# A two-layer hybrid step on one core: the recurrent unit's branch is computed two tiles ahead, and at attention's end an output cast moves between two key casts and more of the projection is offered early

## The chip, the cores and the metric

One core of a Trainium2 chip. The metric is the device time of one execution in microseconds (us), as the median of several runs.

## What is computed

The reference is one inference step through two layers on 640 tokens of width 1024, of which 512 are latent tokens on a grid of 8 rows by 64 columns and 128 are prompt tokens. Layer 0 mixes by neighbourhood attention with 16 heads of 64 (latent queries also read 256 cached and the prompt's keys in one softmax; the prompt attends to itself); layer 1 mixes by a recurrent unit. Behind each mixer comes a feed-forward of width 2816, ahead of each part a root-mean-square norm with a shift and a scale from the conditioning, and behind it a gated add to the residual.

The recurrent unit, per channel of 1024, is:

```
y  = gelu(x @ wi_gate)
xr = x @ wi_branch;  xc = conv4(xr)            # centred, depthwise, bias
r, i = sigmoid(gate matrices (128x128 blocks) @ xc), for both directions
a  = exp(-8 r softplus(-lam));  b = sqrt(1 - a^2) * (i * xc)
h  = a * h + b      # one scan forward, one backward, from given states
out = (y * (h_fwd + h_bwd)) @ wlo
```

## The kernel before

**Precision and chunks.** Every large product is made of float32 numbers split in two: a high part (a cast to the reduced type, on ScalarE) and a low part (the remainder, a subtraction on VectorE). For each of eight slices k of the contraction three matmuls are issued: high by high (line 221), high by low (222), low by high (223). The tokens lie along the free axis, in two halves (320 and 320, or 384 and 256 in the recurrent unit), so a chunk, that is one output tile of 128 channels by one half, is 24 matmuls (`chunk` and `some`). The order in which the engines get their instructions is decided when the program is built, by a scheduler that starts from the order of the code; `pin` sets an instruction behind another.

**Weights and banks.** `unit` loads a weight tile (`raw`), casts it (line 180, `whi` or `whx`) and subtracts (line 182, `wlo` or `wlx`). In the recurrent unit the high part comes by a DMA on the POOL queue. `pg` hands out the accumulators: three banks `mm`, and, where a stage has `mx` banks, those at two of every five calls (`ng % 5` of 1 or 3). So each call of `pg` shifts the turn for all later ones. `ps` gives a named bank, and the stage's first one where the name isn't there.

**Attention's end.** The heads go in eight pairs p. While p = 6 is attended, `qk` makes queries and keys of pair 7: `QS` and `KS` are casts (line 799), one for each head of the pair, and `KZ` the key's remainder (line 800). Behind these the output `O` of the pairs 0 to 6 is split into `ohi` and `olo` (`split`, lines 1313 and 1315), and TensorE begins the output projection (`project`, with `ahead`), three chunks of it early, in slices that fill the waits of the last softmax. That softmax runs through line 830 (scores with their bias and maximum), 833 (exponent), 837 and 839 (scale), 842 (transposes to `tp`), 844 (copies) and 922 (output `op`); for the prompt through 859 to 872. Line 929 copies `op` to `O`. Slice 7 of the output is split last.

**The recurrent unit.** Eight tiles f of 128 channels. `lru_xr` makes the branch in two chunks and copies it, with columns ahead of rows, to one of two buffers `xr` (line 1251). `lru_a` runs the convolution (its first tap on ScalarE, line 1259, three more on VectorE, line 1261) to one of two buffers `xc`, then the gate matrices on TensorE in four pieces (line 1271, `gp`, two buffers), each followed by a tanh that frees its banks (line 1272, ScalarE). `lru_b` makes the coefficients: exponent and tanh (1283, 1284), square root (1285), products (1286, 1287). `lru_c` scans in both directions (1296) and adds the two (1303, 1304). `lru_gate` makes the gate in two chunks and its gelu (1323 to 1327). `lru_d` multiplies (1308) and splits the result (1313, 1315). Tanh, root and gelu are in different tables, so ScalarE loads a table at each turn (ACT_TABLE_LOAD). The loop over t issues `lru_a` of tile t, the branch of t + 1, `lru_b` of t − 1, `lru_c`, the gate and `lru_d` of t − 2.

**The second feed-forward.** Its norm has a second statistic: ones times squares on TensorE (543, 546, tile `at`), variance on VectorE (548), a power on GpSimd (550), a diagonal matrix on VectorE (552), and its spread over the partitions by TensorE into an `mx` bank (560). Around it stand the feed-forward's first chunks (lines 1142 to 1144).

Of the kernel before, what the change touches and what calls it, by code (L numbers as in the profile page):

```python
# [125 lines left out]
class _Step:  # L126
# [467 lines left out]
    def project(self, w, hi, lo, gk, nxt=None, done=None, ahead=False):  # L594
        G = self.need(self.gcols, gk)
        for f in range(KT):
            u = self.unit(w[f], "m" if ahead else None)
            for t0, t1 in CH:
                self.residual(f, t0, t1, self.chunk(u, hi, lo, t0, t1, not ahead or f > 1), G, nxt)
                if nxt:  # L600
                    self.scale(f, t0, t1, *nxt)
            if done:
                done(f)
        if nxt:
            self.stats()
            self.shift(*nxt)
# [173 lines left out]

    def qk(self, p, hi, lo, ap, Q=None, K=None):
        nc = self.nc
# [12 lines left out]
        for S, v, lo in pairs if p else pairs[::-1]:  # L795
            for a in range(2):
                hp = slice(a * HD, a * HD + HD)
                op = slice(HD - a * HD, P - a * HD)
                cast = nc.scalar.copy(S[hp, a], v[hp]).ins
                low = nc.vector.tensor_tensor(lo[a][hp], v[hp], S[hp, a].bitcast(F32), ALU.subtract).ins  # L800
                queue = nc.gpsimd if p in (0, 7) else nc.sync
                queue.dma_start(S[op, a].bitcast(F32), Q[hp] if v is Q else S[hp, a].bitcast(F32))
        self.parted = low, cast
        return QS, KS, KZ
# [448 lines left out]

    def lru_a(self, f, lp):
        nc, xr = self.nc, self.xrs[f % 2]
        gw = self.t([P, 2, 2, P], F32, "gw", 2, lp)
        nc.sync.dma_start(gw, self.i["wg"][f])
        xc = self.t([P, LW], F32, "xc", 2, lp)
        nc.scalar.activation(xc, xr[:, 0:LW], AF.Identity, scale=self.col("cw0", f), bias=self.col("cb", f))
        for j in range(1, 4):  # L1260
            nc.vector.scalar_tensor_tensor(xc, xr[:, j:j + LW], self.col(f"cw{j}", f), xc, ALU.mult, ALU.add)

        def lt():
# [74 lines left out]
    def run(self):  # L1338
# [35 lines left out]
        with self.phase("attn", tp=2, sp=2, op=1, quota=24) as ap:  # L1374
# [10 lines left out]
            for p in range(8):  # L1385
# [3 lines left out]
                new = []  # L1389
                self.attend(p, *QK, V, O, ap, (lambda: new.extend(self.qk(7, xhi, xlo, ap))) if p == 6 else None)  # L1390
                if p == 5:
# [5 lines left out]
                if p == 6:  # L1397
                    ohi = self.big()
                    olo = self.big()
                    for k in range(KT - 1):  # L1400
                        self.split(ohi[:, k], olo[:, k], O[:, k], self.parted)
# [21 lines left out]
        with self.phase("lru", at=1) as lp:  # L1423
            A, B, C, G = {}, {}, {}, {}
            self.xrs = [self.t([P, 648], F32, f"xr{j}", 1, lp) for j in range(2)]
            for xr in self.xrs:
# [61 lines left out]
```

## Time and profile before

| | |
|---|---|
| median of three runs | 1521.86 us (1520.55 to 1522.31) |
| the profiled execution | 1522.37 us |
| its span | 1520.6 us |
| TensorE (PE) busy | 1491.2 us, 98% of the span |
| VectorE (DVE) busy | 1061.5 us, 70% |
| ScalarE (ACT) busy | 698.1 us, 46% |
| GpSimd (POOL) busy | 261.4 us, 17% |
| attention's end (slices of the output projection between the last scores) | about 290 to 320 us of the span |
| recurrent unit's tiles | about 905 to 1030 us |

A row of the order of events holds its start, its length, the engine, the line, the operation, the tile written and the tiles read, the shape, and the count of instructions merged in it; in brackets the idle time of that engine before it, with the engine, tile and line that ended it. The idle time of PE is what counts here. PEclk in a window is the mean clock that TensorE was granted, as a share of full speed. The length of a row holds the pipeline's run-out too, so the next row may start before it is over.

### The profile page before, as it was taken

The numbers are of one execution on the slowest core, as the hardware profiler recorded it, in microseconds if no ns is written. First come the engines' busy times: TensorE is split into PE (matmuls) and PEld (weight loads), VectorE is DVE, ScalarE is ACT, GpSimd is POOL, SyncE is SP. The second block draws the span as 40 slices with busy tenths as digits, with TensorE's granted clock in tenths as the row PEclk, the third lists the DMA queues.
The fourth block names the chain that finished last, engine by engine and source line by source line (L and its number), as shares of the span: only waits on it lengthen the run. The fifth ranks groups of instructions, "written<-read, shape, count | busy, mean of one in ns | idle before, by whom it ended". The sixth has DMA issues, their size and how long they took to land. (4 is left out here: it accounts for less than half of the span.)

```text
span 1520.6 us, 26116 instructions
## 1 busy us (share of the span) xinstructions
PE 1491.2 (98%) x10373; PEld 1441.8 (95%) x10373; DVE 1061.5 (70%) x2005; ACT 698.1 (46%) x1268; POOL 261.4 (17%) x276
## 2 busy tenths in 40 slices
PE   8999999999999999999999999899999999999997
PEld 5999999889999999999999887799999999999997
DVE  5778998679999997434443769876975655566555
ACT  4676766654332123312321478764644342434243
POOL 0112132100111110000000014230232323222211
PEclk9999999999999999999999999999999999999999
DMA  9644665446556664222222543316242231323211
GB/s 375 174 143 160 186 189 167 117 139 194 176 185 195 207 196 132 62 84 84 65 73 83 150 134 102 119 59 216 70 156 80 74 111 57 100 67 97 71 56 70
DMA packets 72330, 196.65 MB, mean 129 GB/s; under 512 B 8048, under 2 KB 24592, under 8 KB 72080
## 3 DMA queue, kind: packets, MB, share of 16 engines
q1 hardware_dynamic: 57392, 142.32, 29.6%
q0 software_dynamic: 14240, 51.98, 11.1%
q8 instruction: 81, 1.33, 0.4%
q10 hardware_dynamic: 576, 0.68, 0.1%
q14 instruction: 41, 0.34, 0.1%
HBM read 179.48 MB, written 8.92 MB: 124 GB/s over the span
## 5 line engine op out<-in xcount | busy, mean ns | idle before, releaser
L221 PE MATMUL mm<-big,whi 128*128 128x320 f32 (+3 forms) x1233 | 383.9, 313 | 4.0 <-ACT big L1313 2.8
L222 PE MATMUL mm<-big,whi 128*128 128x320 f32 (+3 forms) x1233 | 384.2, 312 | 1.7 <-DVE big L1315 1.3
L223 PE MATMUL mm<-big,wlo 128*128 128x320 f32 (+3 forms) x1233 | 384.1, 312 | 0.2 <-DVE wlo L182 0.2
L221 PEld LDWEIGHTS mm<-big,whi 128*128 128x128 f32 x1233 | 233.0, 189 | 6.7 <-ACT big L1313 3.5
L222 PEld LDWEIGHTS mm<-big,whi 128*128 128x128 f32 x1233 | 233.6, 189 | 3.8 <-DVE big L1315 2.2
L223 PEld LDWEIGHTS mm<-big,wlo 128*128 128x128 f32 x1233 | 233.2, 189 | 1.6 <-DVE wlo L182 0.4
L250 DVE SCALAR_TENSOR_TENSOR mprod<-mraw,csb 128x1024 f32<-128x1024 f32 x160 | 194.9, 1218 | 11.8 <-DMA mraw<-in_wm 11.4
L590 DVE SCALAR_TENSOR_TENSOR x<-mm,G,x 128x320 f32<-128x320 f32 (+2 forms) x192 | 77.8, 435 | 82.4 <-PE mm L223 82.3
L180 ACT CAST whi<-raw 128x1024 fp32r<-128x1024 f32 (+1 forms) x71 | 73.9, 1041 | 113.9 <-PE mm L222 65.6
L182 DVE TENSOR_TENSOR wlo<-raw,whi 128x1024 fp32r<-128x1024 f32 (+1 forms) x87 | 105.9, 1218 | 28.7 <-ACT whi L180 16.5
L221 PE MATMUL mm<-big,whx 128*128 128x320 f32 (+3 forms) x348 | 108.4, 311 | 0.0
L223 PE MATMUL mm<-big,wlx 128*128 128x320 f32 (+3 forms) x348 | 108.0, 310 | 0.0
L222 PE MATMUL mm<-big,whx 128*128 128x320 f32 (+3 forms) x348 | 107.9, 310 | 0.0
L246 POOL DMA_DIRECT2D mraw<-in_wm x80 | 43.0, 537 | 358.6 <-DVE mprod L250 266.0
L221 PE MATMUL mx<-big,whi 128*128 128x320 f32 (+3 forms) x287 | 89.5, 312 | 0.0
L223 PE MATMUL mx<-big,wlo 128*128 128x320 f32 (+3 forms) x287 | 88.9, 310 | 0.0
L222 PE MATMUL mx<-big,whi 128*128 128x320 f32 (+3 forms) x287 | 88.7, 309 | 0.0
L221 PE MATMUL mx<-big,whx 128*128 128x320 f32 (+3 forms) x260 | 80.6, 310 | 0.0
L223 PE MATMUL mx<-big,wlx 128*128 128x320 f32 (+3 forms) x260 | 80.5, 310 | 0.0
L180 ACT CAST whx<-raw 128x1024 fp32r<-128x1024 f32 (+1 forms) x40 | 41.1, 1029 | 85.9 <-PE mm L222 47.3
L222 PE MATMUL mx<-big,whx 128*128 128x320 f32 (+3 forms) x260 | 80.3, 309 | 0.0
L1313 ACT CAST whi<-raw 128x1024 fp32r<-128x1024 f32 (+1 forms) x41 | 41.3, 1008 | 70.3 <-PE mm L222 45.2
(347 smaller groups left out, 3725.3 us busy)
## 6 DMA issues: line engine op xcount, KB each, us to landing
raw<-in_gu SPq DMA_DIRECT2D x88, 512.0 KB, 3.5
mraw<-in_wm POOLq DMA_DIRECT2D x80, 512.0 KB, 3.9
raw<-in_dn SPq DMA_DIRECT2D x24, 512.0 KB, 3.6
sw<-in_wm SPq DMA_DIRECT2D x16, 512.0 KB, 10.7
raw<-in_wqk SPq DMA_DIRECT2D x16, 512.0 KB, 4.8
raw<-in_wi SPq DMA_DIRECT2D x16, 512.0 KB, 3.5
whi<-in_wi POOLq DMA_DIRECT2D x16, 512.0 KB, 3.9
raw<-in_dn SPq DMA_DIRECT2D x16, 448.0 KB, 3.3
```

The lines of the kernel that those rows point to most:

```text
L180: nc.scalar.copy(hi, raw)
L182: nc.vector.tensor_tensor(lo, raw, hi.bitcast(F32), ALU.subtract)
L221: nc.tensor.matmul(ps, hi[:, k], xhi[:, k, s], start=(k == 0), stop=False)
L222: nc.tensor.matmul(ps, hi[:, k], xlo[:, k, s], start=False, stop=False)
L223: self.done = nc.tensor.matmul(ps, lo[:, k], xhi[:, k, s], start=False, stop=(k == last)).ins
L246: nc.gpsimd.dma_start(w, self.i["wm"][l * 6 + j - 2, f])
L250: nc.vector.scalar_tensor_tensor(prod, w, 1.0, self.csb[:, s], ALU.mult, ALU.mult, accum_out=out[:, s, f:f + 1])
L590: self.nc.vector.scalar_tensor_tensor(xs, ps[:, a - t0:b - t0], G[:, s, f:f + 1], xs, ALU.mult, ALU.add)
L1313: self.nc.scalar.copy(hi, v)
```

## The change

It has three parts. At attention's end `qk` casts and subtracts slice 0 of the output between the two key casts of pair 7 (the splits of the slices 1 to 6 keep their place), and `project` loads three weight tiles first and treats five half outputs as early in place of four, of which two take `mx` banks. In the recurrent unit the convolution leaves `lru_a` and becomes `lru_conv`; `xr` and `xc` have three buffers, and the loop's round t makes the convolution of t + 1 and the branch of t + 2. And the first feed-forward's stage names its banks in another order, `mx` ahead of `rr`, which changes which old banks they take.

```diff
     def project(self, w, hi, lo, gk, nxt=None, done=None, ahead=False):
+        us = [self.unit(w[f], "m") for f in range(3 if ahead else 0)]
         for f in range(KT):
-            u = self.unit(w[f], "m" if ahead else None)
-            for t0, t1 in CH:
-                self.residual(f, t0, t1, self.chunk(u, hi, lo, t0, t1, not ahead or f > 1), G, nxt)
+            if f == len(us):
+                us.append(self.unit(w[f], "m" if ahead else None))
+            for c, (t0, t1) in enumerate(CH):
+                early = ahead and 2 * f + c < 5
+                ps = self.ps("mx")[:, 0:t1 - t0] if early and 2 * f + c > 2 else self.pg(not early)[:, 0:t1 - t0]
+                self.some(us[f], hi, lo, t0, t1, ps, range(us[f][0].shape[1]))
+                self.residual(f, t0, t1, ps, G, nxt)
...
-                cast = nc.scalar.copy(S[hp, a], v[hp]).ins
+                with self.pin(self.opened if a and S is KS and p == 7 else None):
+                    cast = nc.scalar.copy(S[hp, a], v[hp]).ins
                 low = nc.vector.tensor_tensor(lo[a][hp], v[hp], S[hp, a].bitcast(F32), ALU.subtract).ins
...
+                self.parted = low, cast
+                if p == 7 and S is KS and a == 0:
+                    ohi, olo = self.outs = self.big(), self.big()
+                    with self.pin(cast):
+                        self.opened = nc.scalar.copy(ohi[:, 0], O[:, 0]).ins
+                    with self.pin(low):
+                        nc.vector.tensor_tensor(olo[:, 0], O[:, 0], ohi[:, 0].bitcast(F32), ALU.subtract)
...
-                    for k in range(KT - 1):
+                    for k in range(1, KT - 1):
                         self.split(ohi[:, k], olo[:, k], O[:, k], self.parted)
...
-        with self.phase("ffn0", at=2, rr=1, mx=2, wx=2, quota=56) as fp:
+        with self.phase("ffn0", at=2, mx=2, rr=1, wx=2, quota=56) as fp:
...
-        xr = self.xrs[f % 2]
+        xr = self.xrs[f % 3]
...
+    def lru_conv(self, f, lp):
+        nc, xr = self.nc, self.xrs[f % 3]
+        xc = self.t([P, LW], F32, "xc", 3, lp)
         nc.scalar.activation(xc, xr[:, 0:LW], AF.Identity, scale=self.col("cw0", f), bias=self.col("cb", f))
         for j in range(1, 4):
             nc.vector.scalar_tensor_tensor(xc, xr[:, j:j + LW], self.col(f"cw{j}", f), xc, ALU.mult, ALU.add)
+        return xc
...
+            xc = self.lru_conv(0, lp)
             for t in range(KT + 2):
                 if t < KT:
-                    A[t] = self.lru_a(t, lp)
+                    A[t] = self.lru_a(t, lp, xc)
+                if t == 0:
+                    x1[1]()
                 if t + 1 < KT:
-                    for step in self.lru_xr(t + 1, xhi, xlo) if t else x1[1:]:
+                    xc = self.lru_conv(t + 1, lp)
+                if t + 2 < KT:
+                    for step in self.lru_xr(t + 2, xhi, xlo):
                         step()
```

Line numbers of the changed kernel are higher: by 6 at the keys (799 is 805), by 12 in the softmax and the second feed-forward (830 is 842, 1142 is 1154), by 10 in the convolution (1261 is 1271), and by 16 from there to the end of the unit's code (1272 is 1288, 1286 is 1302, 1308 is 1324, 1313 is 1329). The output's split in `qk` has lines 813 and 815.

How the order of instructions moves, at three places. First ScalarE at attention's end, before (`KS` the keys' cast, `big` from `big` a slice of the output, `S` the softmax):

```order
L833 ACTIVATE S_3758,sm_3761<-S_3758,nm_3759 128x512
L799 CAST KS_3724<-K_3660 64x960 x2
L1313 CAST big_3854<-big_568 128x640
L837 ACTIVATE S_3758<-S_3758,rc_3763 128x512
L1313 CAST big_3854<-big_568 128x640 x5
```

And now:

```order
L845 ACTIVATE S_3762,sm_3765<-S_3762,nm_3763 128x512
L805 CAST KS_3724<-K_3660 64x960
L813 CAST big_3734<-big_568 128x640
L805 CAST KS_3724<-K_3660 64x960
L849 ACTIVATE S_3762<-S_3762,rc_3767 128x512
L1329 CAST big_3734<-big_568 128x640 x5
```

The output's first cast stands ahead of the second key cast; the softmax's scale stays behind all three.

Second, VectorE in the recurrent unit, before: the round that follows a square root, with the product with the gate at line 1308 (`lt` from `lt` and `gl`):

```order
L1286 SCALAR_TENSOR_TENSOR lt_10099<-lt_10345,lt_10099 128x1286
L1261 SCALAR_TENSOR_TENSOR xc_10428<-xr_1597_9509,cols_61,xc_10428 128x643
L1308 TENSOR_TENSOR lt_10178<-lt_10178,gl_10363 128x640
L1287 TENSOR_TENSOR lt_10100<-lt_10100,lt_10099 128x1286
L182 TENSOR_TENSOR wlo_10641<-raw_10638,whi_10640 128x1024
```

And now, where the product is line 1324:

```order
L1302 SCALAR_TENSOR_TENSOR lt_10163<-lt_10414,lt_10163 128x1286
L1271 SCALAR_TENSOR_TENSOR xc_10516<-xr_1598_9510,cols_61,xc_10516 128x643
L182 TENSOR_TENSOR wlo_10645<-raw_10642,whi_10644 128x1024
L1303 TENSOR_TENSOR lt_10164<-lt_10164,lt_10163 128x1286
L1271 SCALAR_TENSOR_TENSOR xc_10516<-xr_1598_9510,cols_61,xc_10516 128x643
L1312 SCALAR_TENSOR_TENSOR lt_10164<-lt_10414,cols_61,lt_10164 128x512
L1312 SCALAR_TENSOR_TENSOR lt_10164<-lt_10414,lt_10164 128x128
L1312 SCALAR_TENSOR_TENSOR lt_10164<-lt_10414,cols_61,lt_10164 128x512
L1312 SCALAR_TENSOR_TENSOR lt_10164<-lt_10414,lt_10164 128x128
L1324 TENSOR_TENSOR lt_10247<-lt_10247,gl_10432 128x640
```

The product, on which ScalarE's next cast waits, moved from behind one step of the next tile's chain to behind all of them and its four scans.

Third, TensorE at the second feed-forward's norm, before (of the statistic its last two rows; 15 matmuls of lines 1142 to 1144 stand between it and line 560, of which five are shown):

```order
L543 MATMUL at_11455<-ones_72,ssq_10993 128x128
L546 MATMUL at_11455<-ones_72,sq_11452 128x128
L1142 MATMUL mm_11538<-big_10856,whi_11483 128x320
L1143 MATMUL mm_11538<-big_10856,whi_11483 128x320
L1144 MATMUL mm_11538<-big_10856,wlo_11484 128x320
L1142 MATMUL mm_11538<-big_10856,whi_11483 128x320
L1143 MATMUL mm_11538<-big_10856,whi_11483 128x320
```

And now:

```order
L543 MATMUL at_11459<-ones_72,ssq_10997 128x128
L546 MATMUL at_11459<-ones_72,sq_11456 128x128
L560 MATMUL mx_11472<-dg_11470,ones_72 128x128 x3
L1154 MATMUL mx_11542<-big_10860,whi_11487 128x320
L1155 MATMUL mx_11542<-big_10860,whi_11487 128x320
```

The same chunk has an `mx` bank in place of an `mm` bank, and stands behind line 560 as a whole.

More of the change, by code (lines that the diff above doesn't have):

```diff
@@ L779, in keys_tile, with qk @@
         return K, ek
-    def qk(self, p, hi, lo, ap, Q=None, K=None):
+    def qk(self, p, hi, lo, ap, Q=None, K=None, O=None):
         nc = self.nc
@@ L1261, in lru_a @@
             nc.vector.scalar_tensor_tensor(xc, xr[:, j:j + LW], self.col(f"cw{j}", f), xc, ALU.mult, ALU.add)
+        return xc
+    def lru_a(self, f, lp, xc):
+        nc = self.nc
+        gw = self.t([P, 2, 2, P], F32, "gw", 2, lp)
+        nc.sync.dma_start(gw, self.i["wg"][f])
         def lt():
@@ L1389, in run @@
                 new = []
-                self.attend(p, *QK, V, O, ap, (lambda: new.extend(self.qk(7, xhi, xlo, ap))) if p == 6 else None)
+                self.attend(p, *QK, V, O, ap, (lambda: new.extend(self.qk(7, xhi, xlo, ap, None, None, O))) if p == 6 else None)
                 if p == 5:
@@ L1397, in run @@
                 if p == 6:
-                    ohi = self.big()
-                    olo = self.big()
-                    for k in range(KT - 1):
+                    ohi, olo = self.outs
+                    for k in range(1, KT - 1):
                         self.split(ohi[:, k], olo[:, k], O[:, k], self.parted)
@@ L1424, in run @@
             A, B, C, G = {}, {}, {}, {}
-            self.xrs = [self.t([P, 648], F32, f"xr{j}", 1, lp) for j in range(2)]
+            self.xrs = [self.t([P, 648], F32, f"xr{j}", 1, lp) for j in range(3)]
             for xr in self.xrs:
```

6 lines of the change are left out of this document (removed).

## The prediction

> **What bounds the kernel now.** I read the page first, for the engine that is the bound; then TensorE's waits over the whole span, for the places where the bound is not kept; then windows of ten us around those places, for the clock; then the order of events there, engine by engine. The page's first part settles the bound:
>
> ```profile
> PE 1491.2 (98%) x10373; PEld 1441.8 (95%) x10373; DVE 1061.5 (70%) x2005; ACT 698.1 (46%) x1268; POOL 261.4 (17%) x276
> ```
>
> The change adds no matmul and removes none, so only TensorE's idle time and its clock can move the total. Of its waits from 60 to 1505 us, four groups matter here (total, times, longest, in us):
>
> ```profile
> PE mm L221 <- ACT big L1313: 2.8, 3, 1.6
> ...
> PE gp L1271 <- ACT lt L1285: 2.2, 1, 2.2
> ...
> PE gp L1271 <- DVE xc L1261: 1.7, 1, 1.7
> ...
> PE at L543 <- DVE ssq L530: 1.7, 1, 1.7
> ```
>
> The first lies at attention's end (0.83), at the recurrent unit's end (1.6) and later; the next two in the recurrent unit; the fourth in a place that the change leaves alone. The windows show what a wait can bring besides (columns: length, busy us of PE, PEld, DVE, ACT, POOL, then the granted clock):
>
> ```profile
> 290.00:300.00 10.00, 8.04 (x44) 7.68 (x45) 9.60 (x19) 8.24 (x18) 5.38 (x8) 0.83 0.67 160
> ...
> 910.00:920.00 10.00, 8.14 (x42) 5.95 (x40) 10.00 (x12) 7.45 (x10) 10.00 (x2) 0.89 0.37 107
> ...
> 980.00:990.00 10.00, 8.30 (x31) 6.30 (x32) 9.97 (x11) 5.30 (x7) 1.45 (x3) 0.83 0.34 108
> ```
>
> A mean clock of 0.83 over ten us is 1.7 us of full-speed work lost, over and above the wait. Such a loss follows the waits at 293, 917 and 982 us (the one at 917 runs on into the next ten us), while the waits of 1.7 at line 543 and at line 1261 and the 1.6 at 1024 us drew none. So in this trace a wait of about 1.8 us or more costs itself and 1.7 more, and a shorter one only itself.
>
> **Attention's end.** These are the three engines there:
>
> ```profile
> 287.84 2.01 ACT L799 CAST KS<-K 64x960 fp32r<-64x960 f32 x2 [0.43 <-DVE K L778]
> ...
> 289.24 1.14 DVE L800 TENSOR_TENSOR KZ<-K,KS 64x960 fp32r<-64x960 f32 x1
> ...
> 289.87 0.72 ACT L1313 CAST big<-big 128x640 fp32r<-128x640 f32 x1
> ...
> 290.31 0.67 DVE L830 CUSTOM_DVE_ANT_0 S<-sp,bt 128x512 f32<-128x512 f32 x1
> ...
> 290.65 0.70 PE L221 MATMUL mm<-big,whi 128*128 128x320 f32 x3 [0.83 <-ACT big L1313]
> ...
> 292.53 1.56 DVE L1315 TENSOR_TENSOR big<-big,big 128x640 fp32r<-128x640 f32 x2
> ...
> 293.41 0.63 PE L222 MATMUL mm<-big,whi 128*128 128x320 f32 x1 [1.31 <-DVE big L1315]
> ```
>
> The output's first cast now stands between the two key casts: the first of these ends near 288.85, the output's 0.72 later at 289.6, and line 221 can start at 289.8 instead of 290.65. That alone only moves the idle time, since the transposes behind it wait for a softmax scale on ScalarE that keeps its place. What counts is the low part: on VectorE it now follows the second line 830 (290.31 and 0.67), ends near 291.8, and line 222 can start near 292.1 instead of 293.41. The second low part is late next, behind the second key remainder (1.14) and a reduction, near 293.9: about 0.5 of the 1.3 is given back there. Gain 0.8, and the idle time from 289.8 falls from 2.1 to about 1.3, under what drew a slow clock here, so the 1.7 at 293 goes as well. Bounds: 0 and 3.0.
>
> At the very end, attention's last softmax is what TensorE waits for:
>
> ```profile
> 314.66 0.49 DVE L929 COPY big<-op 128x128 f32<-128x128 f32 x2 [0.85 <-PE op L922]
> ...
> 317.89 0.63 PE L842 MATMUL tp<-ident,S 128*128 128x128 f32 x4 [1.19 <-DVE S L839]
> ...
> 319.77 0.98 PE L922 MATMUL op<-PT,big 128*64 128x128 f32 x12 [0.46 <-ACT PT L872]
> ```
>
> The latent scale moves ahead of this copy, the prompt's reductions behind both. The first wait here shrinks, the last grows by about the one copy (0.49). I charge 0.5; bounds −0.5 and 1.2. Together attention's end gives −0.8 − 1.7 + 0.5 = −2.0.
>
> The "five half outputs" do not do in the order what the words say: the two added chunks, in banks of the old score buffers, stand on TensorE behind the last `op`, not ahead of it. Two of their matmuls move before the last head pair's pieces, and before, a whole chunk already covered the last cast. Worth 0. One weight split runs one modulation product (1.2 us) later on VectorE, and its first reader comes behind two whole chunks of 24 matmuls.
>
> **The recurrent unit.** First the wait at 917:
>
> ```profile
> 913.40 0.93 ACT L1259 ACTIVATE xc<-xr,cols 128x643 f32<-128x643 f32 x1 [0.80 <-DVE lt L1273]
> ...
> 914.23 0.46 ACT L1323 COPY gl<-mm 128x384 f32<-128x384 f32 x1
> ...
> 917.48 2.29 PE L1271 MATMUL gp<-xc,gw 128*128 128x512 f32 x4 [1.86 <-ACT lt L1272]
> ```
>
> The third `xc` buffer takes away the 0.80; a pair of `xr` copies stands where the gate's copy (0.46) stood, some 0.3 longer. The wait becomes about 1.4 and its slow clock goes: −0.5 − 1.7. With the convolution one tile early, the waits of 1.7 (line 1261) and 2.2 (filed under line 1285; the tap that ends at 981.6 was last) go, and the slow clock at 982 with the second: −1.7 − 2.2 − 1.7.
>
> What is late next is ScalarE's cast of a finished tile, which stands in its queue ahead of a tanh that frees a `gp` bank. Before, the product with the gate stood early on VectorE; now it stands behind the next tile's root products, a weight split, two taps and the four scans:
>
> ```profile
> 965.02 0.88 DVE L1261 SCALAR_TENSOR_TENSOR xc<-xr,cols,xc 128x643 f32<-128x643 f32 x1
> ...
> 965.82 0.82 DVE L1308 TENSOR_TENSOR lt<-lt,gl 128x640 f32<-128x640 f32 x1
> ...
> 966.56 1.49 DVE L1287 TENSOR_TENSOR lt<-lt,lt 128x1286 f32<-128x1286 f32 x1
> ...
> 967.97 1.22 DVE L182 TENSOR_TENSOR wlo<-raw,whi 128x1024 fp32r<-128x1024 f32 x1
> ...
> 969.84 1.28 DVE L1296 TENSOR_TENSOR_SCAN lt<-lt,cols,lt 128x512 f32<-128x512 f32 x1
> ...
> 972.84 1.22 DVE L1303 TENSOR_TENSOR lt<-lt 128x64 f32<-128x64 f32 x2
> ```
>
> From start to start: two root products of 1.41, two taps of 0.80, the split 1.2, the scans 3.0, the product 0.74: 9.4 us from root to cast. From the cast to the next root, ScalarE's own queue:
>
> ```profile
> 966.67 0.73 ACT L1313 CAST big<-lt 128x640 fp32r<-128x640 f32 x1 [3.38 <-DVE lt L1308]
> ...
> 967.31 0.83 ACT L1251 COPY xr<-mm 128x64 f32<-128x64 f32 x2
> ...
> 971.78 0.80 ACT L1272 ACTIVATE lt<-gp,l_hb 128x643 f32<-128x643 f32 x1
> ...
> 980.92 1.28 ACT L1325 ACT_TABLE_LOAD   x1
> ...
> 983.41 0.80 ACT L1272 ACTIVATE lt<-gp,l_hb 128x643 f32<-128x643 f32 x1 [0.40 <-PE gp L1271]
> ```
>
> Cast 0.64; from the tanh to the end of the root 980.92 − 971.78 = 9.1; the `xr` copies, which now lie in this stretch, 0.9: 10.6. In tile 7's round the gate's table and two gelus lie there instead of those copies, 983.41 − 0.40 − 980.92 = 2.1: 11.8. Two rounds are 20.0 + 21.2 = 41.2 us. TensorE's round is read from the starts of two tiles:
>
> ```profile
> 927.48 2.33 PE L1271 MATMUL gp<-xc,gw 128*128 128x512 f32 x8
> ...
> 945.20 2.40 PE L1271 MATMUL gp<-xc,gw 128*128 128x512 f32 x8
> ```
>
> 17.7 us with nine of the short 256-column matmuls fewer than the changed order has per tile, so near 18.8, and 37.6 for two. ScalarE falls 3.6 behind, less the lead with which it enters, which is between 0 and the 3.38 that it idles in the row above. I take a lead of 1.0: 2.6 us of waiting, most of it before tile 7's third `gp`; bounds 0 and 3.6. At the unit's end the last `gp` stands eight chunk matmuls later, so the last cast comes later against the matmuls that cover it: 0.8 on top of the 1.6 there, bounds 0 and 1.0. The unit: −2.2 − 5.6 + 2.6 + 0.8 = −4.4.
>
> **The second feed-forward's start.** The change draws the shared chunk banks in another turn, and from there on the banks alternate differently. At one place this moves a wait to the front:
>
> ```profile
> 1075.29 0.40 PE L1142 MATMUL mm<-big,whi 128*128 128x320 f32 x1
> ...
> 1075.83 0.15 DVE L548 TENSOR_SCALAR var<-at 128x3 f32<-128x3 f32 x1
> ...
> 1076.06 0.85 POOL L550 TENSOR_TENSOR rs<-var,mhalf 128x3 f32<-128x3 f32 x1 [21.70 <-DVE var L548]
> ...
> 1076.94 0.56 DVE L552 TENSOR_TENSOR dg<-ident,rs 128x384 f32<-128x384 f32 x1 [0.96 <-POOL rs L550]
> ...
> 1077.64 0.91 PE L560 MATMUL mx<-dg,ones 128*128 128x128 f32 x6
> ```
>
> Fifteen matmuls from 1075.29 to 1077.6 hid the norm's chain of variance, power and diagonal. Now that chunk takes an `mx` bank, and stands behind line 560, which takes one too. TensorE waits from 1075.3 to 1077.6: +2.3, bounds 2.0 and 2.5. It is longer than the waits that drew a slow clock above, so I add 1.7 (bounds 0 and 1.7).
>
> Here a rule of the notes bears on the sum. The rows say that idle times of 1.9 and 2.2 us were followed by a slow clock. The Trainium skill ("TensorE: Matmul & The Clock Gate", section "HAM oscillation — how this bites in real kernels") allows gaps up to about 3.4 us. By it the new wait would draw no slow clock and the sum would be 1.7 lower. The trace disagrees at 917 and 982, so I keep the 1.7 in the forecast.
>
> **The sum.** −2.0 − 4.4 + 2.3 + 1.7 = −2.4. The profiled execution took 1522.37 (its span 1520.6 and 1.8 around it), so it would become 1520.0. It lies 0.5 above the median of the runs, 1521.86; the three runs spread by 1.76, one slow clock more or less. Against the median the forecast is **1519.5**. A change of 0.2%, 3.04 us, is about what a measurement can tell from none: below 1518.8 is faster, above 1524.9 slower.
>
> **The rivals.** *ScalarE keeps up* (faster): its lead is 3.4 or the rounds overlap, and the 2.6 never shows. Then −5.0, 1516.9; without the slow clock at line 560 also, 1515.2. For it: ScalarE idles 3.38 for one cast before. Against: the cast's chain has grown to 9.4 on VectorE.
>
> *No slow clock behind line 560* (faster): −4.1, 1517.8. For it: its wait of 2.3 may straddle two stretches over which the clock is judged, as the 1.7s were not punished; the page's rule named above would say so. Against: the rows at 917 and 982.
>
> *A slow clock at the `gp` wait too* (no change): the 2.6 falls in one piece, +1.7, 1521.2. For it: it is as long as any here. Against: it builds up over two rounds.
>
> *The weight split waits inside the chain* (slower). The split now stands between root and cast, and its buffer is freed by TensorE:
>
> ```profile
> 979.57 1.23 DVE L182 TENSOR_TENSOR wlo<-raw,whi 128x1024 fp32r<-128x1024 f32 x1 [2.85 <-PE mm L223]
> ```
>
> If it waits 2.85 in each of the two rounds, ScalarE and then TensorE lose 5.7 more: −2.4 + 5.7 = +3.3, 1525.2. It turns the sign to slower from 2.7 a round on. Against: it came to that wait early, with VectorE idle; in the new order VectorE arrives later.
>
> **How the numbers follow.** Forecast 0.33 (own range 1518.0 to 1521.0, 0.07 of it below 1518.8); ScalarE keeps up 0.22; no slow clock behind line 560 0.15; slow clock at `gp` 0.18; split in the chain 0.12, 0.11 of it beyond the bound. Faster 0.22 + 0.15 + 0.07 = 0.44, slower 0.11, the same 0.45. Cases of more than one sign hold most of the chance, so the range reaches from the low end of the first rival, 1515.2, to the third with the unit's end at its bound and the unknown of attention's end, 1522.8; the slower rival and a little on the other side stay out.
>
> **What the profile after would show.** Right: line 222 at attention's end 1.2 to 1.9 us earlier and a clock of 1.00 there; no wait for `xc` after 920 us; waits of `gp` for a tanh of line 1288 in the last two tiles; one wait of about 2.3 at line 560, named after `dg`, and a clock near 0.83 behind it. Wrong: a slow clock still behind line 222 or 917; `gp` waits that repeat in every tile or not at all; line 560 without a wait; any new wait in the first feed-forward.

## The result, and the profile after

Ten runs of the changed kernel took 1525.35 us in the median (1522.60 to 1528.24), ten of the kernel before on the same chip 1519.88 (1515.12 to 1524.14). The ratio is 1.0035, its 95% interval 1.0023 to 1.0047: slower by some 5.3 us, where the forecast was a gain of 2.4, and outside its range. The three runs that the forecast started from are the first three of these ten; their median, 1521.86, lies 2.0 above that of all ten. The profiled execution of after took 1527.98 (span 1526.2), 2.6 above its median; that of before, 1522.37, lay 2.5 above the median of these ten. One later run of before, slow at 1805 us and a granted clock of 0.75, is left out of the ratios and spreads below.

TensorE's work is what it was; the difference is idle time and clock:

```profile
PE 1491.9 (98%) x10373; PEld 1442.7 (95%) x10373; DVE 1061.8 (70%) x2005; ACT 697.2 (46%) x1268; POOL 250.9 (16%) x279
```

To find the stage, take the start of the same matmul in both traces at three marks: the first feed-forward's norm (line 560), the end of the recurrent unit (543) and the kernel's tail (`at<-dg`). Of before, then of after:

```profile
837.02 0.83 PE L560 MATMUL rr<-dg,ones 128*128 128x128 f32 x6
...
1048.35 0.39 PE L543 MATMUL at<-ones,ssq 128*128 128x128 f32 x2
...
1503.86 0.91 PE L679 MATMUL at<-dg,ones 128*128 128x128 f32 x6 [1.26 <-DVE dg L658]
```

```profile
835.25 0.83 PE L560 MATMUL rr<-dg,ones 128*128 128x128 f32 x6
...
1047.89 0.38 PE L543 MATMUL at<-ones,ssq 128*128 128x128 f32 x2
...
1509.46 0.91 PE L684 MATMUL at<-dg,ones 128*128 128x128 f32 x6 [1.26 <-DVE dg L663]
```

After is 1.77 ahead at the first mark, 0.46 ahead at the second and 5.60 behind at the third. So the stretch with attention's end gained 1.8 (forecast 2.0), the recurrent unit lost 1.3 (forecast a gain of 4.4), and the second feed-forward lost 6.1 (forecast 4.0). TensorE's waits of after over the same stretch as in the prediction (total, times, longest) say where:

```profile
PE gp L1287 <- ACT lt L1288: 5.9, 4, 3.5
PE mm L1154 <- DVE g L1116: 2.5, 1, 2.5
PE mm L221 <- ACT xr L1263: 2.4, 2, 1.9
PE mx L560 <- DVE dg L552: 2.1, 1, 2.1
PE mm L221 <- ACT big L1329: 1.7, 1, 1.7
```

The wait at line 560 was forecast (2.3). Those for `g` and for `xr` were not, and that for `gp` is larger than said.

**Attention's end** went as forecast. TensorE there, and the window with its clock:

```profile
290.91 0.66 PE L854 MATMUL tp<-ident,S 128*128 128x128 f32 x4 [0.97 <-ACT S L849]
...
291.58 0.36 PE L222 MATMUL mm<-big,whi 128*128 128x320 f32 x1
...
293.67 0.41 PE L222 MATMUL mm<-big,whi 128*128 128x320 f32 x1 [0.55 <-DVE big L1331]
```

```profile
290.00:300.00 10.00, 8.54 (x56) 8.19 (x57) 9.11 (x19) 7.86 (x18) 4.88 (x7) 1.00 0.65 147
```

Line 222 starts at 291.58 in place of 293.41, the second low part gives 0.55 of it back (forecast 0.5), and the clock is 1.00 in place of 0.83.

**The recurrent unit.** ScalarE's casts of two finished tiles in after, then GpSimd and VectorE ahead of the first:

```profile
954.53 0.73 ACT L1329 CAST big<-lt 128x640 fp32r<-128x640 f32 x1 [7.75 <-DVE lt L1324]
...
974.32 0.73 ACT L1329 CAST big<-lt 128x640 fp32r<-128x640 f32 x1 [4.77 <-DVE lt L1324]
```

```profile
939.44 4.12 POOL L1314 COPY st<-lt 128x1 f32<-128x1 f32 x1 [0.46 <-ACT xr L1263]
943.50 1.05 POOL L178 DMA_DIRECT2D whi<-in_wi  x2
```

```profile
947.34 1.23 DVE L182 TENSOR_TENSOR wlo<-raw,whi 128x1024 fp32r<-128x1024 f32 x1 [3.02 <-issue]
```

ScalarE idles 7.75 and 4.77 us ahead of the casts: the product with the gate comes late, as the prediction said it might. Part of the 7.75 is a thing that it did not see. The scan's last state is copied by GpSimd (`st<-lt`, 128 numbers, line 1314 here); beside a busy VectorE one such copy took 4.12. Behind it in GpSimd's queue stands the DMA of the weight's high part. It went out at 943.5, and VectorE, whose split of that weight now stands in the chain between root and product, waited 3.02 for it. That it was this DMA is read from the order of the rows, since the row itself names no releaser (`issue`); the kernels below without these copies on GpSimd have no such wait between 900 and 985 us.

What TensorE waits for there, and the clock:

```profile
961.26 0.39 PE L221 MATMUL mm<-big,whi 128*128 128x256 f32 x1 [1.89 <-ACT xr L1263]
...
979.53 1.35 PE L1287 MATMUL gp<-xc,gw 128*128 128x512 f32 x4 [0.79 <-ACT lt L1288]
...
988.34 1.35 PE L1287 MATMUL gp<-xc,gw 128*128 128x512 f32 x4 [3.49 <-ACT lt L1288]
```

```profile
960.00:970.00 10.00, 8.74 (x44) 7.50 (x45) 6.30 (x6) 9.49 (x15) 0.53 (x1) 0.83 0.41 127
...
980.00:990.00 10.00, 6.51 (x36) 5.46 (x35) 5.53 (x6) 9.91 (x14) 0.00 (x0) 1.00 0.23 87
```

The wait at 917 of before is 1.43 here, with a clock of 1.00 from 910 to 930, as forecast. The last wait of the unit is 1.65 (1.57 before), and a clock of 0.83 follows it from 1020 to 1030, where before had 1.00.

**The second feed-forward.** The two waits, the windows round them, and what stands ahead of the second on VectorE and GpSimd:

```profile
1077.19 0.91 PE L560 MATMUL mx<-dg,ones 128*128 128x128 f32 x6 [2.11 <-DVE dg L552]
...
1105.18 0.41 PE L1154 MATMUL mm<-xt,whx 128*128 128x320 f32 x1 [2.45 <-DVE g L1116]
```

```profile
1070.00:1080.00 10.00, 7.89 (x59) 7.73 (x58) 7.92 (x14) 4.97 (x7) 0.85 (x1) 1.00 0.51 175
...
1100.00:1110.00 10.00, 7.55 (x41) 7.28 (x40) 10.00 (x18) 4.09 (x8) 2.62 (x3) 0.83 0.49 148
```

```profile
1093.52 0.48 DVE L1019 TENSOR_TENSOR x<-x 128x320 f32<-128x320 f32 x1
...
1095.01 1.58 DVE L1019 TENSOR_TENSOR x<-x 128x320 f32<-128x320 f32 x1
```

```profile
1094.70 1.54 POOL L1075 TENSOR_TENSOR sum<-raw 128x512 f32<-128x512 f32 x1
```

The wait at 560 drew no slow clock (1.00). The one for `g`, 0.5 before and 2.45 now, did (0.83). That `g` stands behind a row of subtractions on VectorE, and one of 0.48 takes 1.58 while GpSimd sums weights; the trace of before has such rows too, so they say why `g` is late and not why it is later now. The Trainium skill ("SBUF — State Buffer", section "Who interferes with whom") says that a VectorE instruction with two inputs in SBUF contends with a GpSimd instruction that reads SBUF; the trace agrees by these rows.

### The profile page after: what moved, and what is told of

Same layout as the page of the kernel before. It is cut to its first block, busy times and chain, and to the rows that moved or that the text cites. A ratio compares the mean times of both kernels' runs of the same rounds, so it can differ in the third digit from the quotient of the medians.

```text
span 1526.2 us, 26120 instructions
## 1 busy us (share of the span) xinstructions
PE 1491.9 (98%) x10373; PEld 1442.7 (95%) x10373; DVE 1061.8 (70%) x2005; ACT 697.2 (46%) x1268; POOL 250.9 (16%) x279
## 5 line engine op out<-in xcount | busy, mean ns | idle before, releaser
L221 PE MATMUL mm<-big,whi 128*128 128x320 f32 (+3 forms) x1215 | 378.6, 313 | 4.7 <-ACT xr L1263 2.4
L222 PE MATMUL mm<-big,whi 128*128 128x320 f32 (+3 forms) x1215 | 378.6, 312 | 0.9 <-DVE big L1331 0.7
L223 PE MATMUL mm<-big,wlo 128*128 128x320 f32 (+3 forms) x1215 | 378.4, 312 | 0.4 <-DVE wlo L182 0.4
L221 PEld LDWEIGHTS mm<-big,whi 128*128 128x128 f32 x1215 | 229.2, 189 | 7.1 <-ACT xr L1263 3.0
L222 PEld LDWEIGHTS mm<-big,whi 128*128 128x128 f32 x1215 | 230.1, 189 | 3.1 <-DVE big L1331 1.2
L223 PEld LDWEIGHTS mm<-big,wlo 128*128 128x128 f32 x1215 | 229.8, 189 | 1.8 <-DVE wlo L182 0.6
L590 DVE SCALAR_TENSOR_TENSOR x<-mm,G,x 128x128 f32<-128x128 f32 (+3 forms) x190 | 77.3, 436 | 88.0 <-PE mm L223 88.0
L221 PE MATMUL mm<-big,whx 128*128 128x320 f32 (+3 forms) x358 | 111.4, 311 | 0.0
L223 PE MATMUL mm<-big,wlx 128*128 128x320 f32 (+3 forms) x358 | 111.1, 310 | 0.0
L222 PE MATMUL mm<-big,whx 128*128 128x320 f32 (+3 forms) x358 | 110.8, 310 | 0.0
L221 PE MATMUL mx<-big,whi 128*128 128x320 f32 (+3 forms) x305 | 94.8, 311 | 0.4 <-ACT big L1329 0.4
L223 PE MATMUL mx<-big,wlo 128*128 128x320 f32 (+3 forms) x305 | 94.2, 309 | 0.0
L222 PE MATMUL mx<-big,whi 128*128 128x320 f32 (+3 forms) x305 | 94.1, 308 | 0.0
L221 PE MATMUL mx<-big,whx 128*128 128x320 f32 (+3 forms) x250 | 77.7, 311 | 0.0
L222 PE MATMUL mx<-big,whx 128*128 128x320 f32 (+3 forms) x250 | 77.3, 309 | 0.0
```

Source lines behind the costliest of these rows:

```text
L221: nc.tensor.matmul(ps, hi[:, k], xhi[:, k, s], start=(k == 0), stop=False)
L222: nc.tensor.matmul(ps, hi[:, k], xlo[:, k, s], start=False, stop=False)
L223: self.done = nc.tensor.matmul(ps, lo[:, k], xhi[:, k, s], start=False, stop=(k == last)).ins
L590: self.nc.vector.scalar_tensor_tensor(xs, ps[:, a - t0:b - t0], G[:, s, f:f + 1], xs, ALU.mult, ALU.add)
```

## The experiments

The theory after the two traces: three things add up, attention's end (a gain of 1 to 2), the branch (a loss, by late weights or by the late product with the gate), and the turn of the shared banks (a loss of 4 to 6 in the second feed-forward). All ratios below are to the kernel before on the same chip, with 95% intervals; one per cent of them is 15.2 us.

**The turn of the banks.** The two chunks that take `mx` banks by name no longer draw from the turn, which shifts it by two for all later calls. Put back alone:

```diff
-                ps = self.ps("mx")[:, 0:t1 - t0] if early and 2 * f + c > 2 else self.pg(not early)[:, 0:t1 - t0]
+                if early and 2 * f + c > 2:
+                    self.ng += 1
+                    ps = self.ps("mx")[:, 0:t1 - t0]
+                else:
+                    ps = self.pg(not early)[:, 0:t1 - t0]
```

> The changed kernel with one line more, which lets the two chunks in old banks count in the turn of the shared banks, so that everything behind the projection draws the banks that it drew before. Theory (the turn of the banks is the loss): the wait of 2.1 at line 560 and the growth from 0.55 to 2.45 of the wait for g in the second feed-forward go, with the slow clock of 1.7 and the 0.4 behind them: 6 us faster than the change, near 1519.2, within 1 us of the kernel before. Rival (the recurrent unit's chain is the loss): 1 to 2 us faster than the change, near 1524.

Measured: 1523.71 us, 1.0018 (1.0005 to 1.0031). That is 2.6 us better than the change by the ratios, between what the theory and the rival expected. From the unit's end to the tail its trace takes 456.4 us, as before (455.5), where after takes 461.6; but its recurrent unit, the same code as in after, took 215.4 where after's took 212.6. The opposite edit, the kernel before with only the turn shifted at the end of the projection:

```diff
+        if ahead:
+            self.ng -= 2
```

> The kernel before, with the count that gives out the banks set back by two after the attention's projection, and nothing else: the shift that the change brings along, alone. Theory: the waits of 2.1 at line 560 and of 2.5 to 2.7 for g come as in the change, with a slow clock behind in a part of the runs: 4 to 5.5 us slower than before, 1523.5 to 1525. Rival (the shift costs something only behind the other two parts): within 1.5 us of before.

Measured: 1524.94, 1.0031 (1.0019 to 1.0043), 4.7 us. Its waits in the second feed-forward, and its two windows:

```profile
PE mm L1144 <- DVE g L1106: 2.2, 1, 2.2
PE mx L560 <- DVE dg L552: 2.1, 1, 2.1
```

```profile
1070.00:1080.00 10.00, 7.88 (x46) 7.72 (x45) 6.32 (x16) 4.64 (x12) 0.85 (x1) 0.83 0.59 196
...
1100.00:1110.00 10.00, 8.18 (x56) 8.18 (x57) 9.47 (x16) 6.28 (x11) 1.87 (x2) 1.00 0.57 171
```

The wait at 560 comes with the turn and with nothing else: it is 2.1 to 2.2 in the four traces with the shifted turn (after, this one and two that follow) and at most 0.2 in the other eleven. The wait for `g` does not: it is 1.4 to 2.7 in those four, and 0.5 to 1.9 in the eleven. From the unit's end to the tail the four take 460.0 to 461.6, the eleven 455.5 to 458.5. The slow clock is behind the other one of the two waits here.

**Attention's end, with the branch as before.** In the first of these the recurrent unit is that of before, in the second the turn is put back too, and the third is the kernel before with only slice 0's cast and remainder between the key casts. The edit of the first and second:

```diff
-        xr = self.xrs[f % 3]
+        xr = self.xrs[f % 2]
...
-            xc = self.lru_conv(0, lp)
...
-                    A[t] = self.lru_a(t, lp, xc)
-                if t == 0:
-                    x1[1]()
+                    A[t] = self.lru_a(t, lp)
...
```

> The changed kernel with the recurrent unit of the kernel before. Theory (turn of the banks): the unit alone costs 1 to 1.5 us, so 1524 to 1524.5. Rival (the unit's chain): near 1519. In the profile the waits for a tanh of line 1288 at 979 and 988 us and for the copy of line 1263 at 961 go, and those of 1.9, 1.7 and 2.2 of the kernel before come back; the wait at line 560 stays near 2.1.

> Both at once: the change at attention's end and in the projection's start alone, with the recurrent unit and the turn of the banks of the kernel before. Theory and rival alike: the gain of 1.9 us read at the first feed-forward remains to the end, near 1518.0, 0.13% faster than before. If attention's gain is given back later, within 0.5 us of before.

> The kernel before with nothing but the output's cast and remainder of slice 0 put between the two key casts. If, as forecast, the fifth half output and the early weights are worth nothing, this equals the run with attention's whole change within 0.5 us, near 1518.0. Rival: the offered chunks bring part of the gain; then this is near 1519, and the last op of attention ends later than with them.

Measured: 1522.69, 1.0013 (0.9998 to 1.0028); 1518.75, 0.9993 (0.9982 to 1.0004); 1518.37, 0.9990 (0.9977 to 1.0003). The first fell between what the theory and the rival expected. The turn, between the first two, is 3.9 us by the medians and 3.0 by the ratios. Attention's end by itself is worth 1.1 to 1.5 us by the ratios, and both intervals hold 1.0, so it can't be told from nothing. The cast alone does as well as the whole: of the early half outputs and of the other order of the bank names nothing shows. The second one's trace holds more. Its waits in the unit, whose code is that of before:

```profile
PE gp L1287 <- ACT lt L1288: 2.5, 3, 1.9
PE mm L221 <- ACT big L1329: 1.6, 1, 1.6
PE gp L1287 <- issue: 1.2, 1, 1.2
```

The wait for `xc` (1.7), which the prediction took from the profile of before, is not there; the matmul that waited 2.2 for the root waits 1.2 (the row filed under `issue`), and the slow clock at 982 is not there either. From line 560 of the first feed-forward to the unit's end this execution takes 206.0, where the profiled one of before took 211.3. In the other two with the old branch and such a short unit (207.2 with the cast alone, 207.1 with the turn alone) the `xc` wait is 0.3 and 0.2, the root's 1.4 and 1.6, and no slow clock follows. The first kernel's trace (212.4) has both waits again, 1.8 and 2.2, with the slow clock. So of those 5.6 us some 4 belong to some executions, not to the kernel.

**The copies and the late product.** Both on the changed kernel with the turn put back: the copies of the last state on VectorE, and the scans of a tile set behind the product of the tile ahead of it.

```diff
-            nc.gpsimd.tensor_copy(st, h[:, d, e:e + 1])
+            nc.vector.tensor_copy(st, h[:, d, e:e + 1])
```

```diff
-                nc.vector.tensor_tensor_scan(hv, av, hv, init, ALU.mult, ALU.add)
+                with self.pin(self.gated):
+                    nc.vector.tensor_tensor_scan(hv, av, hv, init, ALU.mult, ALU.add)
...
-        self.nc.vector.tensor_tensor(y, y, G, ALU.mult)
+        self.gated = self.nc.vector.tensor_tensor(y, y, G, ALU.mult).ins
...
+            self.gated = None
```

> The run with the turn restored, and the sixteen copies of the scan's last state (128x1 each) moved from GpSimd to VectorE, so that no work on GpSimd stands ahead of the weight's DMA in its queue. Theory (the weight split in the chain waits for a DMA that stands behind a copy which GpSimd takes 5 to 11 us for while VectorE is busy): VectorE's waits of 3.8 and 3.9 before line 182 go, ScalarE's wait of 12 for the gate's product falls to about 8, TensorE's of 6.2 for the copy of line 1267 to 2 or less: 3 to 5 us faster than with the turn alone, 1519 to 1520.5. Rival (VectorE's chain is too long in itself): within 1 us of it, near 1523.5.

> The run with the turn restored, and the four scans of a tile pinned behind the gate's product of the tile before, so that the cast's wait is some 3.8 us shorter (scans 3.0, a tap 0.8). Theory (the DMA behind GpSimd's copies decides): the split's waits of 3.8 and 3.9 stay, TensorE gains 2 to 3 us, near 1521. Rival (the chain's length): 4 to 5 us faster than with the turn alone, near 1519.

> Turn restored, copies on VectorE and the scans behind the product. Theory and rival alike give a branch two tiles ahead whose cast comes in time: no wait of TensorE for a copy of xr or a tanh between 920 and 985 us, and the unit from its first gate matrices to the next norm's statistic not over the 143 to 145 us of the two runs of attention's change alone: 1516 to 1518. If the unit stays over 148 us there, a third cause is open.

Measured: the copies 1519.39, 0.9988 (0.9977 to 0.9999); the product 1520.64, 0.9998 (0.9983 to 1.0013); both 1514.44, 0.9963 (0.9951 to 0.9976). Against 1.0018 with neither, the two give 0.30% and 0.20%, and together 0.55% (on two chips): they add up, as two causes would, though for the product alone the intervals overlap. The clearest step is from the copies alone to both, on one chip: 0.25% or 3.8 us, with intervals that don't overlap, and the unit takes 205.1 us in place of 209.0 in the two traces. TensorE's waits for `gp` fall from 6.4 to 3.6 there and a slow clock of 3.4 goes, while its other waits grow from 0.4 to 2.1. That edit moves the product ahead of the scans, and with it lets ScalarE's cast pass one tanh and some matmuls change places. With both, the kernel is faster than before and after, more than was expected, and its six runs lie within 3.3 us (1513.71 to 1516.98), where the 10 to 35 of before spread over 7 to 12 on each chip. With both but the turn left as the change has it:

> The change as it is, with the copies on VectorE and the scans behind the gate's product, and with the shifted turn of the banks. Theory: the mended unit without the shift ran at 1514.4, and the shift adds what it added to the kernel before, 4.1: 1518 to 1519. Rival (half of the 4.1 came through the unit's state at its end): 1516 to 1517.

Measured: 1519.52, 1.0005 (0.9994 to 1.0017): the turn again, some 0.42%, or 6 us, between two chips. In their two traces the unit takes the same (205.3 and 205.1), and the stretch behind it 3.3 more.

**Is it the lead, or the copies?** If the copies were the cause of the branch's loss, the old branch should not gain by their removal. Two attempts had the copies moved in the kernel with attention's edits alone (old branch, turn put back), to ScalarE and to VectorE:

```diff
-            nc.gpsimd.tensor_copy(st, h[:, d, e:e + 1])
+            nc.scalar.copy(st, h[:, d, e:e + 1])
```

> Attention's change alone, with the recurrent unit and the turn of the kernel before, and the sixteen copies of the scan's state on ScalarE in place of GpSimd; otherwise the same order on every engine. Theory (GpSimd's copies delay the weights' DMA in the kernel before too, by an amount that differs from run to run): 2 to 4 us faster than with attention's change alone, 1515 to 1517, and its runs lie closer together than the 7 us there. Rival (the delay bites only in the longer chain of the branch two tiles ahead): 1518 to 1519, with the same spread.

> As the run with the copies on ScalarE, but with them on VectorE, behind the scans whose result they take, so that nobody waits for them; the scheduler then also sets the gate pieces of the last tiles later, close to where the branch two tiles ahead has them. It asks what the second tile of lead earns once the copies are gone from GpSimd. Theory (the lead pays only when the cast's chain is short): near the mended unit without the scans pinned, 1518 to 1519.5, and above the mended one at 1514.4. Rival (the copies were all of it): 1514 to 1515.5.

Measured: 1521.65, 1.0020 (1.0008 to 1.0032), and 1523.96, 1.0030 (1.0017 to 1.0042). Both miss what either theory expected, and neither is a clean test. In the first ScalarE waits for the scans, 14.8 us in sum within the unit. In the second the scheduler set the last tile's gate matrices 49 matmuls later, so that less is left to cover the last cast, and TensorE waits 8.1 us for it.

A cleaner test leaves the copies out, and with them the unit's last states, one of the five outputs, which are then zeros. Then no operation of the other four engines changes its place, in either branch:

```diff
-            nc.gpsimd.tensor_copy(st, h[:, d, e:e + 1])
```

> Attention's edits alone (the kernel of attention's end with the branch as before and the banks' turn restored), with GpSimd's sixteen copies of the scans' last state left out; the states' output is set to zero at the start and is not computed. The other four engines' rows stand in the same order as with the copies, so this is the control that the two kernels with moved copies were not. Theory (copies hold up the high weight's DMA, in the old order too, in the longer of its executions): 0.9965 to 0.998 of the kernel before, near 1515.5 where that takes 1519.5, with the spread of the runs cut from 7 us to about 4; line 182 waits no more than 0.5 in the unit. Rival (the copies hurt only the new order, whose chain holds the split): as with the copies, 0.999 to 1.000, near 1518.8, spread as it was.

> The whole change with the banks' turn restored, with the same sixteen copies left out (states set to zero, not computed); the other four engines' rows as with the copies. Theory (the copies are what the new branch loses by, the lead by itself gains or costs little): 3 to 6 us under the same kernel with the copies, 0.998 to 0.9995 of the kernel before, within 2 us of the control on the old branch on either side. Rival 1 (the lead pays once the weights come in time): 2 to 5 us below that control. Rival 2 (the late gate product costs by itself, copies or not): 2 to 5 us above that control, with the waits of line 1291 for line 1292 as large as with copies, 5 us in sum.

Measured: the old branch 1515.00, 0.9978 (0.9966 to 0.9991), the new one 1518.60, 0.9998 (0.9989 to 1.0008). So the copies cost both branches about the same, 0.15% of the old and 0.20% of the new (between chips, with intervals that overlap), and without them the new one is still 3.6 us slower, on one chip, as it is with them (1.0018 against 0.9993, 3.8 us). That is what the second rival expected: the copies are not what the branch loses by. This pair sets the whole new branch against the whole old one; that its loss is the late product is shown by the step above, where the product's place alone was worth 3.8. TensorE's waits in the unit and the windows behind the largest, of the old branch and then of the new one:

```profile
PE gp L1287 <- ACT lt L1288: 2.3, 2, 1.8
PE mm L221 <- ACT big L1327: 1.6, 1, 1.6
PE mm L221 <- ACT gl L1339: 0.2, 1, 0.2
```

```profile
980.00:990.00 10.00, 10.00 (x69) 9.59 (x68) 6.64 (x9) 9.98 (x13) 0.00 (x0) 1.00 0.16 52
```

```profile
PE gp L1291 <- ACT lt L1292: 6.1, 4, 3.5
```

```profile
980.00:990.00 10.00, 6.51 (x21) 4.18 (x20) 7.82 (x8) 9.02 (x12) 0.00 (x0) 0.72 0.17 53
990.00:1000.00 10.00, 10.00 (x70) 10.00 (x69) 6.51 (x9) 9.94 (x14) 0.00 (x0) 0.94 0.17 52
```

Waits of 4.1 against 6.1, and in the new branch 2.8 and 0.6 us of clock lost (the old one's clock stays at 1.00): 5.4 in sum, where the two traces differ by 5.0 between line 560 and the unit's end, and the medians by 3.6. The chain behind the wait of 3.5, new branch without the copies, VectorE and then ScalarE:

```profile
967.19 1.28 DVE L1316 TENSOR_TENSOR_SCAN lt<-lt,cols,lt 128x512 f32<-128x512 f32 x1
...
970.19 0.80 DVE L1326 TENSOR_TENSOR lt<-lt,gl 128x640 f32<-128x640 f32 x1
```

```profile
960.32 1.28 ACT L1305 ACTIVATE lt<-lt 128x1286 f32<-128x1286 f32 x1
...
971.03 0.73 ACT L1331 CAST big<-lt 128x640 fp32r<-128x640 f32 x1 [4.76 <-DVE lt L1326]
...
981.61 1.27 ACT L1305 ACTIVATE lt<-lt 128x1286 f32<-128x1286 f32 x1
```

With the copies on VectorE and the product still late the same cast waits 4.76 too; with the product ahead of the scans it waits about half as long:

```profile
966.49 0.73 ACT L1334 CAST big<-lt 128x640 fp32r<-128x640 f32 x1 [2.29 <-DVE lt L1329]
```

What stays open: whether the lead, once its product is early, is better than the old branch without the copies (0.9963 and 0.9978, on two chips, with intervals that overlap), and how much of the difference is clock rather than wait, which varies from execution to execution.

## Why the prediction was wrong

**Attention's end: the number held, and luck had a part in it.** By the traces it is −1.8 for −2.0, with the clock at 1.00 as said, the 0.5 given back as said, and the half outputs worth nothing as said. But most of it is the slow clock (1.7), and that was not certain in the kernel before. The kernel with the turn alone has attention's end as before, and in its trace the same waits of 0.83 and 1.31 drew none:

```profile
293.87 0.41 PE L222 MATMUL mm<-big,whi 128*128 128x320 f32 x1 [1.31 <-DVE big L1317]
```

```profile
290.00:300.00 10.00, 7.86 (x50) 7.24 (x51) 9.87 (x19) 8.68 (x19) 4.86 (x8) 1.00 0.70 176
```

From the transposes at 288.77 (before), 289.23 (the turn alone) and 288.41 (after) to the first feed-forward's line 560 the three take 548.2, 546.9 and 546.8 us. So against the second of them the edit gained nothing. None of the thirteen traces with the new end has a slow clock there, and one of the two with the old end has: that the edit prevents it is likely, not shown. In the runs it is worth −1.1 to −1.5, with intervals that hold 0.

**The second feed-forward: right in kind, a third of it missed.** "TensorE waits from 1075.3 to 1077.6: +2.3" came out at 2.1. The slow clock came once in each of the four traces with the shifted turn, behind line 560 in two of them and behind the wait for `g` in the other two, after among them. What the step left out is that second wait, which went from 0.5 to 2.45: 2.1 + 1.9 + 1.7 is 5.7 of the 6.1, so the term was 2.1 short. How much of the 1.9 is the turn's stays open, since the wait for `g` reaches 1.9 in a trace without it.

**The recurrent unit: wrong, in two steps.** The first is "the waits of 1.7 (line 1261) and 2.2 … go, and the slow clock at 982 with the second: −1.7 − 2.2 − 1.7". They went, but most of them were not the kernel's to lose: other executions of the same unit have 1.2 to 1.8 of the 3.9 us of waits and no slow clock, and take 4 to 5 less. A gain of 5.6 was counted against an execution that was itself late. The same holds for the 1.7 of clock at 917: in five traces of this unit TensorE waits 1.9 there, and only two of them have the slow clock. The two later waits go with GpSimd's copies: one near 950 us took 3.5 in the two executions of the old branch that have these waits and 1.0 to 1.3 in the three that are short, and without the copies the old branch has neither wait.

The second is "I take a lead of 1.0: 2.6 us of waiting". ScalarE's side of it was exact: 9.4 from root to cast and 11.8 from cast to root, and the last rows above give 971.03 − 961.60 = 9.4 and 982.88 − 971.03 = 11.85. TensorE's round, put near 18.8, is shorter. The starts of two tiles, in the new branch without the copies:

```profile
943.80 2.33 PE L1291 MATMUL gp<-xc,gw 128*128 128x512 f32 x8
...
962.24 2.33 PE L1291 MATMUL gp<-xc,gw 128*128 128x512 f32 x8
```

That is 18.4, so in two rounds ScalarE falls 41.2 − 36.9 = 4.3 behind, not 3.6. The lead was guessed, between 0 and the 3.38 that ScalarE idles before, and there is none: the last tiles wait 0.79 and 3.49 in after, 4.3 in sum. And the clock, set at nothing for this wait, took up to 3.4 more in other executions, so the rival with a slow clock at the `gp` wait came true in those, not in the profiled one.

The term of 0.8 at the unit's end was 0.1, but a slow clock stood behind that wait. In the profiled pair the 5.7 between the forecast for the unit (−4.4) and its result (+1.3) lies about in these: the wait at 961 with its clock (3.6), `gp` (1.7 over the forecast) and the unit's end (1.0 over), 6.3 in sum.

**The rival with the split in the chain** had the right place and a wrong reason. The split did wait, 3.02 in one round; behind it the cast and `xr` came late (1.89 at 961, with a slow clock), a wait that the new branch without the copies does not have. But by the order of the rows it waited for a DMA behind a copy, not for TensorE to free the buffer. It was priced at 5.7 and is worth, with the copies gone, about 3 (0.20%); and as the old branch gains 0.15% by the same, little of it is the change's cost.

So the sum, by the ratios of the runs: attention's end −1.1 to −1.5, the branch with its late product +3.6 to +3.8, the turn +2.6 to +6: +4.7 to +8.7, measured +5.3.

## What to carry to other kernels

Before a wait or a slow clock is booked as a gain, ask whether it belongs to the kernel or to the profiled execution: where the runs spread by as much as the gain, look for the same wait in a second trace. When work is set ahead of a chain, count what the chain's last step now stands behind; here that chain was estimated right to a tenth, and the slack it was set against was a guess. And an edit that changes who draws from a shared turn can move waits wherever the turn is used, so follow it to the end, not to the first place.

## What the runs showed of the hardware

A slow clock is not set by the length of the wait alone, as the prediction's "about 1.8 us or more" had it. The wait of 3.49 in after was followed by a clock of 1.00, the same wait of 3.48 without the copies by 0.72. Of four waits of 2.1 to 2.2 at line 560 two drew a slow clock, and of five waits of 1.9 near 917 us two. Most slow clocks cost about 1.7 us (0.83 over ten us), some twice that (0.72 and 0.94 over two such windows). The thirteen traces with the new attention's end show the size: they take 546.8 to 546.9 us from the transposes to line 560 where a slow clock follows the last softmax, and 545.2 to 545.3 where none does. The Trainium skill ("TensorE: Matmul & The Clock Gate", section "Part 1: The HAM clock gate") describes a window of 3.4 us that runs freely, so that it depends on where work falls in it. The differences between equal waits agree with that; that waits of 1.65 to 2.45, shorter than such a window, can be followed by a slow clock too is what the traces add.

A GpSimd copy of one column took 0.2 to 12.5 us for the same 128 numbers. VectorE was busy all through the long one, and each of the sixteen in after ends within 0.2 us of the end of a VectorE instruction.

```profile
908.60 12.49 POOL L1314 COPY st<-lt 128x1 f32<-128x1 f32 x1
...
995.04 0.18 POOL L1314 COPY st<-lt 128x1 f32<-128x1 f32 x1 [0.46 <-DVE lt L1312]
```

With these copies gone, the twelve runs of the new branch lie within 2.0 us (1517.49 to 1519.45), with them on VectorE within 4.4, where the twelve with them on GpSimd lay within 9.1 (1518.01 to 1527.13): they are a good part of the spread from run to run. In the old branch the spread shrinks less, from 7.2 to 5.6.
